# Moving the sample group's loads and all stores of results and gates from SyncE's queue to GpSimd's

## The chip, the cores and the metric

The kernel runs on one core of a Trainium2 chip. The metric is the device time of one execution in microseconds (us). The kernel before took 2027.31 us, the median of three runs (2026.1 to 2027.38 us).

The core's engines appear under the names of the profile: PE is TensorE (matmuls; PEld is its weight load), DVE is VectorE, ACT is ScalarE, POOL is GpSimd, and SP is SyncE, which computes nothing and here issues nearly all DMA transfers. "SPq" marks a transfer issued by SP. Each engine works through its own list of instructions in order.

## What is computed

One step of a one-layer hybrid decoder, for a prompt of 256 tokens and, with the same weights, 8 samples of one token each: 264 columns in all, with a model width of 2048.

```
h     = rmsnorm(x);  proj = h @ w_in          # three mixers and three merge gates
o_r   = RWKV-7 time mixing   (16 heads x 64)
o_m   = mLSTM matrix memory  (4 heads x 256)
o_g   = gated linear attention, GLA (4 heads, 128 x 256)
gates = sigmoid(proj_gate + gate_b)           # 3 x 2048 per token
x     = x + sum(gates * (o_r, o_m, o_g each @ w_branch)) @ w_out
x     = x + (silu(g) * u) @ ffn_w_down        # g, u = halves of rmsnorm(x) @ ffn_w_gu
y     = rmsnorm(x)
```

For the samples each mixer starts from a state in memory and gives back the state after one token: RWKV S (16 x 64 x 64 per sample), mLSTM C (4 x 256 x 256), GLA S (4 x 128 x 256). All is float32.

## The kernel before, in words

**Weights.** Every matrix is packed on the host into one stream `wst`, cut into units of mostly 4 x 128 rows by 256 columns (512 KB). `weights` loads a unit into `raw` (L331, SP), ScalarE rounds it into `wh` (L334), VectorE makes the remainder `wl = raw - wh` (L257, a helper that records every two-input operation of VectorE). `raw`, `wh` and `wl` have three buffers each. `unit` then issues 24 matmuls for a full unit (L266, also a helper): `wh` times the high part of the activations, `wh` times the low part, `wl` times the high part. These three steps of a weight unit are marked as of high priority.

**Order of the work.** The code is written for Tile, a framework that assigns semaphores and whose scheduler puts the instructions of each engine in order before the kernel runs, by priority (the order in the code, with the marked ones ahead) and by when it expects them to be ready. So an instruction can stand on its engine well before or after its place in the code. On the chip that order is fixed.

**Background work.** The mixers are written as generators. `unit` calls `fill` after each half of a unit; `fill` moves the prompt's mixers on by a step and, every second call (every fourth from the FFN on), one generator of `bg`, the sample group's work. In `fill` the kernel before also issues the stores that have been put on the list `stores` since the last call.

**The transfers that the change touches.**

- `load` (L369, SP): the samples' loads. In the sample stage: `Ss` from the RWKV states, `Ct` from the mLSTM states, `St` from the GLA states (all in six shared buffers, tag `ct`), and `qb` and `gqb`, rows of queries broadcast to all partitions. In the FFN part: `Cb` and `kb` (in new_C), `Sb` and `kgb` (in new_S), `Ss` (in new_W).
- `store`: puts a transfer on the list; `fill` issues it a step later (L379, SP). So go the gates (`g_d` from `sgate`, 24 times), the mixers' outputs (`o_d`), the prompt's new states and small results.
- Stores written out directly (SP): `o_cs`, `o_sh`, `o_cv`, and the samples' new states `o_sC` (L1471), `o_sg` (L1486), `o_swkv` (L1506).

Weight loads, the loads of `of`, `sgl` and `xr` for the merge, the blocks of the RWKV inverse (`nd`, `xd`) and the final `yT` stay on SP.

**Renewing the states.** `later` runs new_C 16 times (four heads, pairs of samples), new_S 16 times, new_W 8 times. A job of new_C: loads `Cb` (three buffers) and `kb` (two); four scaled copies into `kv` on ScalarE (L263; `kv` has two buffers); two fused multiply-adds on VectorE (L260); the store of `kv` to `o_sC`. A job of new_S: loads `Sb` (three buffers) and `kgb` (two); a product into `Sb` on POOL (L1480); four scaled copies into `kvg` on ScalarE; one addition on VectorE; the store to `o_sg`. A job of new_W loads `Ss`, works on it with POOL (L1500, `tms`) and VectorE, and stores it to `o_swkv`.

**Other POOL work.** In the sample stage POOL makes the products `tms` (L860) and, for the prompt's GLA heads, the differences `gd` (L1195), from which ScalarE and VectorE make the operands `gsc` of the score matmuls. In the projection part it copies small pieces, such as `bonS` (L642).

Of the kernel before, what the change touches and what calls it, by code (L numbers as in the profile page):

```python
# [247 lines left out]
def body(tc, a, stop=None):  # L248
    nc = tc.nc
# [3 lines left out]
    def sb(name, bufs=1, **kw):  # L253
        return tc.tile_pool(name=name, bufs=bufs, **kw)

    def tt(out, x, y, op):
        vec.tensor_tensor(out=out, in0=x, in1=y, op=op)  # L257
# [4 lines left out]
    def af(out, x, f, bias=0.0, scale=1.0):  # L262
        act.activation(out=out, in_=x, func=f, bias=bias, scale=scale)  # L263
# [6 lines left out]
    with ctx:  # L270
# [20 lines left out]
        cvT = const.tile([P, 16, 3, B], F32, name="cvT")  # L291
# [5 lines left out]
        sh_o = const.tile([P, 26, 9], F32, name="sh_o")  # L297
        cv_o = const.tile([P, 16, 11], F32, name="cv_o")

        def V(n, i=0, w=1):  # L300
            return vecs[:, VEC[n] + i:VEC[n] + i + w]

        def NVv(n, i=0, w=1):
            o = {"gb": 0, "w0": 48, "a0": 56, "ka": 64}[n] + i
            return nvec[:, o:o + w]
# [57 lines left out]
                unit(name, ps, k0, nk, hi, lo, kof)  # L363
            return ps

        mix, bg, tick, stores, every = {}, [], [0], [], [2]

        def load(out, in_):
            nc.sync.dma_start(out=out, in_=in_)  # L369

        def store(out, in_):

            stores.append((out, in_))

        def fill():

            now, stores[:] = stores[:], []
            for o, i in now:
                nc.sync.dma_start(out=o, in_=i)  # L379
            for lane in list(mix):  # L380
                while mix[lane] and next(mix[lane][0], 0) == 0:
                    mix[lane].pop(0)
                if not mix[lane]:
                    del mix[lane]
            tick[0] += 1
            if tick[0] % every[0] == 0:
                step(1)

        def step(n):
            while n and bg:  # L390
                g = bg.pop(0)
                if next(g, 0) is None:
                    bg.append(g)
                    n -= 1
# [91 lines left out]
        def setup():  # L486

            lw = ip.tile([P, BW], F32, tag="xs", name="lw", bufs=5)
            lgw = ip.tile([64, BW], F32, tag="xs", name="lgw", bufs=5)
            gf = ip.tile([P, len(LV), P], F32, tag="xs", name="gf", bufs=5)  # L490
            for t, n in ((lw, "lw"), (lgw, "lgw"), (cvT, "cvT"), (nT, "nT"), (mT, "mT"), (ga, "ga"), (gf, "gm")):
                nc.sync.dma_start(out=t, in_=a[n])
            for n, w in (("gb", 48), ("w0", 8), ("a0", 8), ("ka", 8)):
                vec.tensor_scalar(out=NVv(n, 0, w), in0=V(n, 0, w), scalar1=-1.0, scalar2=None, op0=MUL)

            for i, src, hh, hl in ((0, lw[H0], H0, H1), (1, lw[H1], H1, H0), (2, lgw, H0, H1)):
                act.copy(out=LW[i][hh], in_=src)
                tt(LW[i][hl], src, LW[i][hh].bitcast(F32), SUB)
            act.activation(out=identR, in_=ones[:, 0:4], func=AF.Copy, scale=0.0)
            for t, n in ((onesR, ones), (bonesR, bones), (cenR, cen), (identR[0:4], ident[0:4, 0:4]), (identR[32:36], ident[32:36, 32:36])):  # L500
                act.copy(out=t, in_=n)
            for j in range(3):
                w = V("cw", 16 * j, 16).unsqueeze(2).to_broadcast([P, 16, B])
                if j == 0:
                    tt(cvS, cvT[:, :, 0, :], w, MUL)
                else:
                    tmp = ip.tile([P, 16, B], F32, name="tmp")
                    tt(tmp, cvT[:, :, j, :], w, MUL)
                    tt(cvS, cvS, tmp, ADD)
            tt(cvS, cvS, V("cb", 0, 16).unsqueeze(2).to_broadcast([P, 16, B]), ADD)  # L510
            nc.sync.dma_start(out=a["o_cs"], in_=cvT[:, :, 1:3, :])
            pool.tensor_copy(out=gm, in_=gf)
            zero = ip.tile([P, 520], F32, name="zero")
            pool.memset(zero, 0.0)
            for q in range(4):
                for i in range(2):
                    nc.sync.dma_start(out=xd[q][i][0:66560].rearrange("(p f) -> p f", p=P), in_=zero)
            ictx.close()
# [535 lines left out]
        def row(t, o, ap):  # L1054

            return bass.AP(tensor=t.tensor, offset=t.offset + o, ap=[[0, P]] + ap)
# [302 lines left out]
        for name, _, _, _ in groups[1:]:  # L1359
            if name[0] == "r" and name[1] == 0:  # L1360
                r_group(name[2])
                if name[2] == 0:
                    mp = mctx.enter_context(sb("m", side="right"))
                    mix.setdefault("m", []).append(m_gates())
            elif name[0] == "m" and name[1] == 0:
                m_group(name[2])
            elif name[0] == "g":
                if gp is None:
                    nc.sync.dma_start(out=a["o_sh"], in_=sh_o)
                    nc.sync.dma_start(out=a["o_cv"], in_=cv_o)  # L1370
                    while mix or stores:
                        fill()
                    rctx.close()
                    mctx.close()
                    gp = gctx.enter_context(sb("g"))
                    sp = gctx.enter_context(sb("s"))
                    bg += [r_sample(), m_sample()]
                g_part(*name[1:])
            elif name[0] == "gate":
                if name in trail:  # L1380
                    break
                gate(*name[1:])
        while mix or bg or stores:
            fill()
        gctx.close()

# [69 lines left out]
        def new_C(h, b):  # L1456
            Cb = fp.tile([P, 2, 2, 256], F32, name="Cb", bufs=3)
            load(Cb, a["mC"][h, :, b:b + 2])
            kb = fp.tile([P, 2, 256], F32, name="kb", bufs=2)
            load(kb, row(rk_d, BW * b + 256 * h, [[BW, 2], [1, 256]]))  # L1460
            yield
            kv = fp.tile([P, 2, 2, 256], F32, name="kv", bufs=2)
            for i in range(2):
                for j in range(2):
                    af(kv[:, i, j, :], kb[:, i, :], AF.Identity, scale=vS[:, 0, 2 * h + j, b + i:b + i + 1])
            yield
            for i in range(2):
                if i:
                    yield
                stt(kv[:, i], Cb[:, i], scS[:, h, b + i:b + i + 1], kv[:, i], MUL, ADD)  # L1470
            nc.sync.dma_start(out=a["o_sC"][h, :, b:b + 2], in_=kv)  # L1471

        def new_S(h, b):
            Sb = fp.tile([P, 2, 2, P], F32, name="Sb", bufs=3)
            load(Sb, a["gS"][h, :, b:b + 2])
            kb = fp.tile([P, 2, 2, P], F32, tag="kb", name="kgb", bufs=2)
            load(kb, row(rg_d, 1536 * b + 384 * h + 128, [[1536, 2], [1, 256]]))
            yield
            kv = fp.tile([P, 2, 2, P], F32, tag="kv", name="kvg", bufs=2)
            pool.tensor_tensor(out=Sb, in0=Sb, in1=kb[:, :, 1:2, :].to_broadcast([P, 2, 2, P]), op=MUL)  # L1480
            for i in range(2):
                for j in range(2):
                    af(kv[:, i, j, :], kb[:, i, 0, :], AF.Identity, scale=vS[:, 1, 2 * h + j, b + i:b + i + 1])
            yield
            tt(kv, kv, Sb, ADD)
            nc.sync.dma_start(out=a["o_sg"][h, :, b:b + 2], in_=kv)  # L1486

        def new_W(v0):
            S = fp.tile([P, 8, 64], F32, tag="Sb", name="Ss", bufs=3)
            load(S, a["wkv"][:, v0:v0 + 8, :])  # L1490

            def along(j):
                return natR[:, j:j + 1, :].to_broadcast([P, 8, 64])

            def col(x):
                return x[:, v0:v0 + 8].unsqueeze(2).to_broadcast([P, 8, 64])

            yield
            tm = fp.tile([P, 8, 64], F32, tag="kb", name="tms", bufs=2)
            pool.tensor_tensor(out=tm, in0=along(5), in1=col(uR), op=MUL)  # L1500
            tt(S, S, along(1), MUL)
            yield
            tt(S, S, tm, SUB)
            tt(tm, along(2), col(natR[:, 3, :]), MUL)
            tt(S, S, tm, ADD)
            nc.sync.dma_start(out=a["o_swkv"][:, v0:v0 + 8, :], in_=S)  # L1506

        def later():
            yield from pipeline(new_C(h, b) for h in range(4) for b in range(0, B, 2))
# [63 lines left out]
```

## Time and profile before

| | us |
|---|---|
| median of three runs | 2027.31 |
| the profiled execution | 2026.99 |
| its span, first to last instruction | 2025.3 |
| PE busy | 1957.6 |
| DVE busy | 1336.6 |
| ACT busy | 1042.1 |
| POOL busy | 166.9 |

The span is what the trace's times count in. Matmuls are pipelined: one of 264 columns shows a duration of some 285 ns, but the next one starts before it ends, so a group's sum of durations says nothing, and the busy time of a stretch divided by its matmuls does. The parts of the kernel follow each other in the span about so: projections with the RWKV and mLSTM mixers of the prompt to 640 us; GLA of the prompt and all mixers of the samples to 950 us; the merge of the branches to 1130 us; the output projection to 1237 us; the FFN to the end. The granted TensorE clock over the whole run is 0.994 of full speed.

### The profile page before, as it was taken

How to read it: one execution, taken by the hardware profiler on the slowest of the kernel's cores; microseconds unless marked ns; L12 is line 12 of the kernel's file. 1: busy time of each engine (PE TensorE's matmuls, PEld its weight loads, DVE VectorE, ACT ScalarE, POOL GpSimd, SP SyncE). 2: the span in 40 equal slices, each digit the busy share in tenths (PEclk: the TensorE clock that was granted, in tenths of full speed). 3: DMA queues.
4: the chain of work that ended last, by engine and by line, in shares of the span. 5: the costliest groups of instructions: out<-in, count | busy, mean ns of one | idle time of the engine just before them, and what ended most of it. 6: DMA issues, size and time to landing. Idle time of an engine off the chain costs nothing.

```text
span 2025.3 us, 41016 instructions
## 1 busy us (share of the span) xinstructions
PE 1957.6 (97%) x16526; PEld 1913.3 (94%) x16526; DVE 1336.6 (66%) x2382; ACT 1042.1 (51%) x1700; POOL 166.9 (8%) x257
## 2 busy tenths in 40 slices
PE   7999999999999899999999999998999999999997
PEld 7899999999998889989999999988999999999997
DVE  7777776767766878776566666568654455555554
ACT  5755655755755355566444566554443344444443
POOL 5110100100100311110000000123000000000000
PEclk9999999999999999999999999999999999999999
DMA  7563554554454778558777898987655555555554
GB/s 256 180 184 128 172 174 142 166 171 151 163 171 145 242 279 275 176 175 271 224 227 221 281 309 303 300 299 260 202 179 177 183 187 180 184 178 185 174 182 137
DMA packets 173526, 414.89 MB, mean 205 GB/s; under 512 B 47512, under 2 KB 69432, under 8 KB 173336
## 3 DMA queue, kind: packets, MB, share of 16 engines
q1 hardware_dynamic: 172904, 411.53, 62.3%
q8 instruction: 129, 2.11, 0.4%
q10 hardware_dynamic: 432, 0.74, 0.1%
q14 instruction: 61, 0.50, 0.1%
HBM read 379.61 MB, written 32.61 MB: 204 GB/s over the span
## 4 chain that ended last, share of the span: by engine, by line
PE 67%; DMA 12%; DVE 9%; ACT 7%; issue 4%; SPq 1%; POOL 1%; DVEq 0%; ACTq 0%; POOLq 0%
PE ps L266 61%; PE mx L266 5%; DVE wl L257 4%; DMA o_sC<-kv 4%; ACT wh L334 3%; DMA kgb<-rg_d 2%; DVE dot L840 1%; DMA of<-o_d 1%; DMA Ss<-wkv 1%; ACT sg L263 1%; DMA raw<-wst 1%; ACT sgate L263 1%; DMA gqb<-rg_d 1%; DMA o_swkv<-Ss 1%; DMA St<-gS 0%
## 5 line engine op out<-in xcount | busy, mean ns | idle before, releaser
L257 DVE TENSOR_TENSOR wl<-raw,wh 128x1024 fp32r<-128x1024 f32 (+2 forms) x613 | 747.9, 1222 | 470.3 <-ACT wh L334 464.9
L334 ACT CAST wh<-raw 128x1024 fp32r<-128x1024 f32 (+2 forms) x613 | 631.9, 1033 | 605.6 <-PE ps L266 521.6
L266 PE MATMUL ps<-xh,wh 128*128 128x264 f32 x2080 | 608.9, 293 | 7.2 <-ACT wh L334 6.9
L266 PE MATMUL ps<-xh,wl 128*128 128x264 f32 x2080 | 596.8, 287 | 16.0 <-DVE wl L257 15.8
L266 PE MATMUL ps<-xl,wh 128*128 128x264 f32 x2080 | 593.9, 286 | 0.0
L266 PE MATMUL ps<-gh,wl 128*128 128x264 f32 x1408 | 401.7, 285 | 13.8 <-DVE wl L257 13.7
L266 PEld LDWEIGHTS ps<-xh,wl 128*128 128x128 f32 x2080 | 393.7, 189 | 21.5 <-DVE wl L257 19.9
L266 PEld LDWEIGHTS ps<-xh,wh 128*128 128x128 f32 x2080 | 395.2, 190 | 12.5 <-ACT wh L334 7.6
L266 PE MATMUL ps<-gh,wh 128*128 128x264 f32 x1408 | 400.7, 285 | 2.1 <-ACT wh L334 2.1
L266 PE MATMUL ps<-gl,wh 128*128 128x264 f32 x1408 | 399.3, 284 | 0.0
L266 PEld LDWEIGHTS ps<-xl,wh 128*128 128x128 f32 x2080 | 395.5, 190 | 0.9
L266 PEld LDWEIGHTS ps<-gh,wl 128*128 128x128 f32 x1408 | 264.3, 188 | 18.9 <-DVE wl L257 18.9
L266 PEld LDWEIGHTS ps<-gh,wh 128*128 128x128 f32 x1408 | 264.9, 188 | 3.3 <-ACT wh L334 3.3
L266 PEld LDWEIGHTS ps<-gl,wh 128*128 128x128 f32 x1408 | 265.1, 188 | 0.0
L266 PE MATMUL ps<-al,wh 128*128 128x264 f32 x704 | 200.3, 285 | 0.0
L266 PE MATMUL ps<-ah,wh 128*128 128x264 f32 x704 | 200.1, 284 | 0.0
L266 PE MATMUL ps<-ah,wl 128*128 128x264 f32 x704 | 199.7, 284 | 0.0
L266 PEld LDWEIGHTS ps<-ah,wl 128*128 128x128 f32 x704 | 133.0, 189 | 0.0
L266 PEld LDWEIGHTS ps<-al,wh 128*128 128x128 f32 x704 | 132.2, 188 | 0.0
L266 PEld LDWEIGHTS ps<-ah,wh 128*128 128x128 f32 x704 | 132.1, 188 | 0.0
L266 PE MATMUL ps<-oh,wh 128*128 128x264 f32 x384 | 109.0, 284 | 0.0
L266 PE MATMUL ps<-oh,wl 128*128 128x264 f32 x384 | 108.9, 284 | 0.0
(406 smaller groups left out, 2366.8 us busy)
## 6 DMA issues: line engine op xcount, KB each, us to landing
raw<-wst SPq DMA_DIRECT2D x579, 512.0 KB, 3.5
raw<-wst SPq DMA_DIRECT2D x32, 384.0 KB, 3.1
Ct<-mC SPq DMA_DIRECT2D x16, 512.0 KB, 5.1
Cb<-mC SPq DMA_DIRECT2D x16, 512.0 KB, 6.7
o_sC<-kv SPq DMA_DIRECT2D x16, 512.0 KB, 6.3
g_d<-sgate SPq DMA_DIRECT2D x24, 264.0 KB, 4.4
sgl<-g_d SPq DMA_DIRECT2D x24, 264.0 KB, 3.6
qb<-rq_d SPq DMA_DIRECT2D x4, 1024.0 KB
```

The source lines that it names most:

```text
L257: vec.tensor_tensor(out=out, in0=x, in1=y, op=op)
L263: act.activation(out=out, in_=x, func=f, bias=bias, scale=scale)
L266: pe.matmul(out, lhsT=lhsT, rhs=rhs, start=start, stop=stop)
L334: act.copy(out=wh[:, 0:nk, :], in_=raw[:, 0:nk, :])
L840: vec.tensor_tensor_reduce(out=tm[:, 0:x.shape[1]], in0=x, in1=y, scale=1.0, scalar=0.0, op0=MUL, op1=ADD, accum_out=out)
```

## The change

`load` issues on GpSimd's queue. `store` is the same function: it issues at once, on GpSimd's queue, and no list is kept. The stores that were written out on SP call `store`.

```
-        mix, bg, tick, stores, every = {}, [], [0], [], [2]
+        mix, bg, tick, every = {}, [], [0], [2]
 
         def load(out, in_):
-            nc.sync.dma_start(out=out, in_=in_)
-
-        def store(out, in_):
-
-            stores.append((out, in_))
+
+            nc.gpsimd.dma_start(out=out, in_=in_)
+
+        store = load
 
         def fill():
 
-            now, stores[:] = stores[:], []
-            for o, i in now:
-                nc.sync.dma_start(out=o, in_=i)
             for lane in list(mix):
...
-            nc.sync.dma_start(out=a["o_cs"], in_=cvT[:, :, 1:3, :])
+            store(a["o_cs"], cvT[:, :, 1:3, :])
...
-                    nc.sync.dma_start(out=a["o_sh"], in_=sh_o)
-                    nc.sync.dma_start(out=a["o_cv"], in_=cv_o)
-                    while mix or stores:
+                    store(a["o_sh"], sh_o)
+                    store(a["o_cv"], cv_o)
+                    while mix:
                         fill()
...
-        while mix or bg or stores:
+        while mix or bg:
             fill()
...
-            nc.sync.dma_start(out=a["o_sC"][h, :, b:b + 2], in_=kv)
+            store(a["o_sC"][h, :, b:b + 2], kv)
...
-            nc.sync.dma_start(out=a["o_sg"][h, :, b:b + 2], in_=kv)
+            store(a["o_sg"][h, :, b:b + 2], kv)
...
-            nc.sync.dma_start(out=a["o_swkv"][:, v0:v0 + 8, :], in_=S)
+            store(a["o_swkv"][:, v0:v0 + 8, :], S)
```

## Rows read from the trace of the kernel before

**Rows 1.** The page's first part: the span, and each engine's busy time.

```profile
span 2025.3 us, 41016 instructions
...
PE 1957.6 (97%) x16526; PEld 1913.3 (94%) x16526; DVE 1336.6 (66%) x2382; ACT 1042.1 (51%) x1700; POOL 166.9 (8%) x257
```

**Rows 2.** Busy us by stretch: length, PE, PEld, DVE, ACT, POOL, clock, DMA, GB/s.

```profile
1500.00:2000.00 500.00, 500.00 (x4119) 500.00 (x4119) 261.24 (x312) 209.33 (x253) 0.00 (x0) 1.00 0.55 181
100.00:640.00 540.00, 538.69 (x5084) 514.86 (x5083) 392.48 (x849) 321.66 (x585) 41.83 (x130) 1.00 0.50 159
640.00:950.00 310.00, 289.63 (x2303) 282.82 (x2303) 234.45 (x602) 159.96 (x303) 51.88 (x52) 0.98 0.71 234
1130.00:1290.00 160.00, 153.75 (x1228) 150.01 (x1227) 106.27 (x150) 98.70 (x176) 0.00 (x0) 1.00 0.91 307
1290.00:1420.00 130.00, 118.43 (x936) 114.43 (x934) 91.85 (x119) 64.82 (x121) 37.80 (x24) 1.00 0.85 281
```

**Rows 3.** Waits, 640 to 950 us: who for whom, us, times, longest.

```profile
PE ps L266 <- DVE wl L257: 9.7, 8, 3.0
PE mx L266 <- DVE gsc L257: 6.1, 5, 3.3
...
ACT wh L334 <- DMA raw<-wst: 29.5, 13, 8.1
```

**Rows 4.** An issue of SP, a piece of the chain, the page's weight loads.

```profile
663.50 0.38 SPq L369 DMA_DIRECT2D qb<-rq_d  x1
...
667.58 7.66 DMA raw<-wst
...
raw<-wst SPq DMA_DIRECT2D x579, 512.0 KB, 3.5
```

**Rows 5.** new_C: a wait, one late store in four timeline rows, the page's median.

```profile
ACT kv L263 <- DMA o_sC<-kv: 39.2, 13, 4.6
...
1200.62 0.74 DVE L260 SCALAR_TENSOR_TENSOR kv<-Cb,scS,kv 128x512 f32<-128x512 f32 x1
...
1209.39 0.33 SPq L331 DMA_DIRECT2D raw<-wst  x1
1209.77 0.42 SPq L1471 DMA_DIRECT2D o_sC<-kv  x1
...
1215.48 0.91 ACT L263 ACTIVATE kv<-kb,vS 128x256 f32<-128x256 f32 x2 [1.67 <-DMA o_sC<-kv]
...
o_sC<-kv SPq DMA_DIRECT2D x16, 512.0 KB, 6.3
```

**Rows 6.** 1290 to 1420 us: a wait of ACT, one of SP, the chain.

```profile
ACT kvg L263 <- DMA kgb<-rg_d: 26.1, 12, 3.5
...
SPq L369 <- DMA o_swkv<-Ss: 12.3, 5, 3.6
...
1318.20 1.24 DVE wl L257
...
1320.36 5.44 DMA kgb<-rg_d
```

**Rows 7.** Cb's issues (ns min/median/max, first and last start), and ACT's first `rs` of the FFN.

```profile
L369 SPq DMA_DIRECT2D Cb<-mC x16: 423/466/857, 1126.5 to 1268.4; - x16
...
1237.17 0.47 ACT L263 ACTIVATE rs<-mx,vecs 128x264 f32<-128x264 f32 x1
```

**Rows 8.** POOL: a small copy (busy us, mean ns), and new_S's products by stretch.

```profile
L642 POOL COPY bonS<-bon 128x8 f32<-128x8 f32 x8 | 7.4, 920 | 2.9 <-DMA raw<-wst 1.6 <-DVE bon L257 0.9
...
1290.00:1380.00 90.00, 22.88 (x16) 1.00 0.88 288
```

**Rows 9.** The dots on DVE (ns min/median/max), and one beside POOL's work.

```profile
L840 DVE CUSTOM_DVE_ANT_0 dot<-Ct,qb x64: 402/414/2616, 679.4 to 810.0; 128x256 f32<-128x256 f32 x64
...
697.65 2.62 DVE L840 CUSTOM_DVE_ANT_0 dot<-Ct,qb 128x256 f32<-128x256 f32 x1
...
696.67 5.84 POOL L860 TENSOR_TENSOR tms<-Ss,natR 128x1024 f32<-128x1024 f32 x2 [6.18 <-DMA Ss<-wkv]
```

## The prediction

> **What bounds the kernel now.** I read the page's first part, then the busy time by stretch, then the waits of the stretches that have idle time, and last SP's issues beside the chain of waits. TensorE is busy for 1957.6 us of a span of 2025.3 us [rows 1]; what can be won is its idle time, and the stretches say where that lies [rows 2]. From 1500 to 2000 us there is none: 4119 matmuls at 500/4119 = 0.121 us. From 100 to 640 us there are 540 - 538.69 = 1.3 us. Three stretches hold the rest that the change can touch, and in all three the moved transfers run beside the weights: the sample stage, 640 to 950 us, idles 310 - 289.63 = 20.4 us; the stretch in which the mLSTM states are renewed (new_C, 1130 to 1290 us) 160 - 153.75 = 6.25 us; that of new_S and new_W (1290 to 1420 us) 130 - 118.43 = 11.6 us. Together 38 us, 1.9% of the time. The remaining 28 us or so stand at the start and the end, where almost nothing is moved.
>
> In the sample stage TensorE waits 9.7 us for `wl` and 6.1 us for the gate scores of GLA; ScalarE waits 29.5 us for raw weights [rows 3]. The longest such wait can be followed [rows 4]: SP issues the 1 MB broadcast `qb` at 663.50; the weight load issued at 667.58 takes 7.66 us on the chain, where the median weight load lands in 3.5 us. It queued behind `qb` on the same queue.
>
> In the new_C stretch ScalarE waits 39.2 us, 13 times, for the store `o_sC` to give back a `kv` buffer [rows 5]. The rows show why the store is late. The second product of a job starts at 1200.62 and is done at 1201.36; its store is issued at 1209.77. In between SP, which works in order, stands at a weight load that it can issue only at 1209.39, when `wl` of an earlier unit has been made. At 1215.48 the store has landed (6.3 us is the median), and ScalarE starts the job that has waited 1.67 us for that buffer. So there is a ring: store lands, `kv` on ScalarE, `wh` behind it, `wl`, the weight load's issue on SP, the next store behind that. One turn takes about 9.5 us and TensorE falls short a little on each.
>
> The third stretch has the same ring with `kgb` in the store's place: ScalarE waits 26.1 us for it, and on the chain a `wl` of 1.24 us stands ahead of a `kgb` load of 5.44 us. In addition SP itself stands 12.3 us at L369, for stores of `o_swkv` to land, with weight loads queued behind [rows 6].
>
> **The change part by part.** *What moves.* By the loops: 108 loads (16 each of Ct, Cb, kb, Sb, kgb, 12 Ss, 8 St, 4 qb, 4 gqb), 77 issues of `store` at L379 (24 of gates among them) and 43 direct stores (16 o_sC, 16 o_sg, 8 o_swkv, o_cs, o_sh, o_cv), 228 in all. An issue holds SP for 0.42 us [rows 5], at the median of Cb 0.466 us [rows 7]; with 0.43 us, 98 us come off SP. I cost that at nothing by itself: SP's time is mostly waiting, and from 1500 to 2000 us, where nothing is moved, it feeds TensorE without a gap.
>
> *What POOL pays.* Before, POOL issues no DMA, so the price of one is bounded: below by SP's 0.43 us, above by 1.43 us, a whole product Sb (22.88/16). I take 0.92 us, a copy of eight elements a partition [rows 8], the nearest POOL instruction whose time is hardly data. That adds 228 x 0.92 = 210 us to POOL's 167 us: 19% of the span in place of 8%. Tightest is new_S, 16 jobs in 90 us [rows 8], 5.6 us each: 1.43 + 3 x 0.92 = 4.2 us, and 5.7 us at the upper price, when POOL is just full.
>
> *New_C.* The store goes out when the product is done: 1201.36 + 0.92, and with 6.3 us to land the buffer is free by 1208.6; ScalarE asks for it at 1213.8 (1215.48 less its wait of 1.67). Slack 5 us even if landing stays as it is; at POOL's upper price 4.7 us. The ring opens. Next late is the `kb` and `Cb` pair, two and three jobs ahead, which SP's weight loads no longer hold. I take 6 of the 6.25 us.
>
> *New_S and new_W.* Opening the ring takes SP's turn (a `wl` and a weight load's issue, 1.24 + 0.33 us) out of a `kgb` turn, and the waits for `o_swkv` leave SP. But `kgb` has two buffers and must still land, and now POOL's own product Sb, which waits for `kgb`, stands ahead of the loads and stores queued behind it. I take 7 of 11.6 us.
>
> *Sample stage.* Weight loads no longer follow 1 MB and 512 KB loads on one queue. Bounds for such a load: 3.5 us, the median, to 7.66 us as now. I take 7 of the 9.7 us. The 6.1 us for GLA's scores stay: they begin on POOL, at `gd`, and some 60 of the moved transfers stand on that queue. Where a store now waits on POOL for ScalarE or VectorE to finish (stores are no longer put off a step), what is queued behind it is `gd` and `tms`, and behind these `gsc` on VectorE and the scores on TensorE. I charge 3 us (bounds 0 to 10: 60 x 0.92 = 55 us of POOL, shared out over 310 us of which POOL works 52), and 2 us for the hand-over to the `of` loads, which need the last stores landed.
>
> *First 640 us and the end.* POOL's small copies and memsets wait behind stores there; the mixers run many steps behind the projections and the idle time is 1.3 us. Without that slack each store would cost its 0.92 us. Nothing moved stands near the end. I take 0, bounds 0 and +5 us.
>
> **Sum**: -6 - 7 - 7 + 3 + 2 = -15 us. The profiled execution took 2026.99 us, 1.7 us beyond its span and 0.3 us under the median of the runs. 2027.31 - 15 gives 2012 us.
>
> What SP does to the store at 1209.77 is 8.4 us of standing in line and 0.42 us of issue [rows 5]; the sum above rests on the first. A rule speaks against a gain: the Trainium skill, "DMA: Bandwidth & Descriptors", section Issuing engines are not separate DMA queues, says that the DMAs of all engines end on the same 16 DMA engines, and that issuing from several saves only issue time. By that rule the sum would be 0, the first rival below.
>
> **The rivals.** *No change.* The landings carry the stalls: in new_C the DMA engines are 91% busy, in new_S and new_W 85% [rows 2]. Half a microsecond more per issue on the rings of 32 new_C and new_S jobs is up to 16 us, which eats the gain. Against it: 8.4 us of the new_C ring are SP's, not the landing's. 2024 to 2031 us, chance 0.15.
>
> *POOL's issuing holds VectorE: slower.* The trace shows that the two hold each other: a `dot`, 414 ns at the median, takes 2.62 us at 697.65 while POOL works on `tms` from 696.67 [rows 9]. If writing a transfer's descriptors does the same for 0.92 us, the 112 moved transfers of 1130 to 1420 us take 103 us of VectorE. It is busy 106.27 + 91.85 = 198 us there [rows 2], so 301 us are wanted in 290: VectorE becomes the bound, 11 us over, and with some 60 transfers in the sample stage (234 + 55 of 310 us) another 5 or so. It decides from (290 - 198)/112 = 0.82 us a transfer. About 2043 us, chance 0.14. Against it: `tms` reads two whole tiles, a DMA issue reads none.
>
> The Trainium skill, "SBUF — State Buffer", section SBUF: two separate sides, lets a VectorE operation with two SBUF inputs exclude only a GpSimd operation that reads SBUF, and warns that VectorE in a two-port mode locks GpSimd out of writing descriptors. By that rule `wl` would not be held; nothing in the trace before tests it.
>
> *A denser order: slower.* The engines' orders come from the framework's scheduler: the first Cb load is issued at 1126.5 us, though the code puts it inside the gate-and-up loop, whose first `rs` runs at 1237.17 [rows 7]. With SP free it may pack one new_C job onto two weight units (2 x 24 x 0.121 = 5.8 us) instead of about three. That is 1.31 MB moved (512, 256 and 512 KB) plus 1.05 MB of weights, 407 GB/s, where 307 GB/s are 91% of the engines: full, 337. So 7.0 us a job, 1.2 us of idle time x 16 = 19 us against 6.25 now, and later landings in new_S. About 2035 us, chance 0.10. Against it: two `kv` buffers and the stores' landing limit the scheduler as well.
>
> **How the numbers follow.** A measurement of this kernel tells about 0.2%, 4 us, from no change. My forecast, 1998 to 2023 us, has 0.61; its lower end is all of 9.7 + 6.25 + 11.6 us won at no cost, 1999.8, and a little of GLA's waits. The range goes on to 2043 us, the second rival's price; what is left out is worse than that, or better than 1998 us. Faster 0.61, within 0.2% 0.15, slower 0.14 + 0.10 = 0.24.
>
> **What would show it.** Right: ScalarE's wait for `o_sC` in new_C falls from 39 us to a few; SP's issues are weight loads and little else; ScalarE's longest wait for raw weights is under 5 us; TensorE idles under 1 us in new_C. Wrong: VectorE's `wl` longer than the 1.24 us of [rows 6] wherever POOL issues; POOL issues of over 1.4 us with `Sb` late; DMA shares above 0.95 with TensorE idle in new_C; or the same wait of ScalarE on a store that was issued in time.

## The result, and the profile after

The changed kernel takes 2087.49 us (median of four runs, 2084.4 to 2093.77) where the kernel before takes 2026.7 us beside it: a ratio of 1.0301, 95% interval 1.0283 to 1.032. It is slower by 61 us; 15 us of gain had been forecast. The profiled execution took 2093.77 us, the slowest of the four.

The page's first part and some of its DMA issues (KB each, median us to landing):

```profile
span 2091.7 us, 41167 instructions
...
PE 1989.6 (95%) x16526; PEld 1944.6 (93%) x16526; DVE 1349.6 (65%) x2382; ACT 1043.6 (50%) x1700; POOL 298.9 (14%) x485
...
raw<-wst SPq DMA_DIRECT2D x579, 512.0 KB, 3.4
...
Ct<-mC POOLq DMA_DIRECT2D x16, 512.0 KB, 10.4
Cb<-mC POOLq DMA_DIRECT2D x16, 512.0 KB, 9.6
o_sC<-kv POOLq DMA_DIRECT2D x16, 512.0 KB, 7.9
```

The span is 66.4 us longer than in [rows 1]. TensorE is busy for 32.0 us more with the same 16526 matmuls, so they ran more slowly, and it idles 102.1 us in place of 67.7. The busy time by stretch, as in [rows 2], says where:

```profile
640.00:950.00 310.00, 282.24 (x2187) 275.12 (x2186) 229.14 (x590) 150.29 (x290) 93.03 (x120) 0.96 0.68 220
...
1130.00:1290.00 160.00, 133.12 (x939) 126.93 (x937) 94.09 (x131) 90.65 (x183) 55.32 (x82) 0.91 0.91 312
1290.00:1420.00 130.00, 109.58 (x794) 106.96 (x795) 88.76 (x112) 53.05 (x89) 42.19 (x54) 0.90 0.68 215
...
1420.00:1700.00 280.00, 280.00 (x2308) 280.00 (x2307) 143.92 (x168) 111.28 (x127) 0.00 (x0) 1.00 0.56 181
```

Count matmuls, which weigh idle time and slow clock alike. The sample stage does 116 fewer than in [rows 2]; new_C, new_S and new_W do 1228 + 936 - 939 - 794 = 431 fewer. At 0.121 us that is 14 and 52 us: the whole 66 us by which the span grew.

**What became of new_C and new_S.** The next view is the busy time of ScalarE's weight casts alone (x counts them), then clock, DMA share and GB/s. First the kernel before, while its stores `o_sC` and then `o_sg` go out:

```profile
1135.00:1285.00 150.00, 48.44 (x47) 1.00 0.90 307
1292.00:1380.00 88.00, 27.51 (x27) 1.00 0.88 290
```

The same two stages in the changed kernel:

```profile
1148.00:1244.00 96.00, 23.81 (x23) 0.89 0.98 359
1244.00:1342.00 98.00, 20.93 (x21) 0.86 0.76 234
```

The work on the samples' states has been packed among fewer weight units, in new_C among half as many. (The stretches take in a cast or two more at their edges than the counts that follow.) In ScalarE's order, which is fixed before the kernel runs, 46 weight casts stand between the first and the last scaled copy into `kv`, and 26 for `kvg`; in the changed kernel 23 and 19. So 16 jobs of new_C pass in 96 us instead of 150, with the DMA engines 98% busy; but the 23 weight units of that time are 23 x 24 x 0.121 = 67 us of TensorE's work, and 29 us are lost there against a TensorE at full speed; in the kernel before 47 such units left 13.5 us of 150. In the 98 us of the second row it is 21 x 24 x 0.121 = 61 us of work, and 37 us are lost.

Three rows of the changed kernel's timeline show that the store is no longer late:

```profile
1159.30 1.41 DVE L260 SCALAR_TENSOR_TENSOR kv<-Cb,scS,kv 128x512 f32<-128x512 f32 x2
...
1161.70 0.56 POOL L370 DMA_DIRECT2D o_sC<-kv  x1
...
1164.70 0.51 ACT L263 ACTIVATE kv<-kb,vS 128x256 f32<-128x256 f32 x1 [5.37 <-DMA o_sC<-kv]
```

The products end at 1160.71, and the store goes out 0.99 us later, where SP had taken 8.4 us [rows 5]. ScalarE waits for an earlier `o_sC` all the same, 5.37 us: the landing has become the wait. The waits from 1140 to 1400 us:

```profile
POOL kb L370 <- ACT kv L263: 51.5, 13, 8.2
...
ACT kvg L263 <- DMA o_sg<-kvg: 40.6, 10, 7.6
...
PE ps L266 <- ACT wh L334: 28.0, 14, 7.4
ACT kv L263 <- DMA o_sC<-kv: 25.5, 8, 5.9
...
PE ps L266 <- DVE wl L257: 19.2, 23, 2.1
```

ScalarE's order has `kv` and `kvg` ahead of the weight casts; it stands at them, and TensorE waits for `wh` behind. In new_S the two `kvg` buffers are given back by `o_sg`, for which before nobody waited.

**The clock.** Busy time by 3 us of the changed kernel; the first x counts matmuls, the clock is third from the right:

```profile
1182.00:1185.00 3.00, 2.76 (x23) 2.55 (x22) 0.00 (x0) 0.08 (x1) 0.00 (x0) 1.00 1.03 421
1185.00:1188.00 3.00, 0.53 (x2) 0.30 (x2) 1.96 (x3) 2.57 (x5) 0.14 (x1) 0.86 1.02 410
1188.00:1191.00 3.00, 2.93 (x13) 2.93 (x14) 2.48 (x5) 2.61 (x6) 1.65 (x3) 0.50 0.88 303
1191.00:1194.00 3.00, 3.00 (x16) 3.00 (x15) 3.00 (x7) 3.00 (x7) 0.00 (x0) 0.50 0.85 200
1194.00:1197.00 3.00, 3.00 (x26) 3.00 (x26) 1.03 (x2) 0.06 (x1) 1.80 (x3) 1.00 1.01 396
```

TensorE did two matmuls in 1185 to 1188 us. Then it was granted 0.50, the lower level of 1.2 GHz, for 6 us, and did 13 and 16 matmuls where 26 fit. So a long stall costs twice. The clock accounts for TensorE's 32 us of extra busy time: it was 0.91 and 0.90 from 1130 to 1420 us, where it had been 1.00, and 0.96 in place of 0.98 in the sample stage, by an estimate 0.09 x 160 + 0.10 x 130 + 0.02 x 310 = 34 us.

**Sample stage.** GpSimd's timeline from 662 us:

```profile
662.51 0.56 POOL L370 DMA_DIRECT2D rk_d<-vr  x1
663.06 0.56 POOL L370 DMA_DIRECT2D Ss<-wkv  x1
663.62 0.50 POOL L370 DMA_DIRECT2D rk_d<-vr  x1
664.11 0.92 POOL L370 DMA_DIRECT2D qb<-rq_d  x1
665.02 0.55 POOL L370 DMA_DIRECT2D Ct<-mC  x1
```

And two pieces of the chain of waits (start, us):

```profile
665.02 13.98 DMA Ct<-mC
699.88 9.24 DMA raw<-wst
```

Loads leave in a bunch as soon as buffers and queue allow. The `Ct` of 665.02 takes 13.98 us to land, and a weight load on its own queue still takes 9.24 us, beside `Ct` and `qb` loads issued in the same microseconds. The waits of the stage, 640 to 950 us:

```profile
PE ps L266 <- DVE wl L257: 13.0, 8, 4.2
PE mx L266 <- DVE gsc L257: 10.3, 5, 3.0
...
ACT wh L334 <- DMA raw<-wst: 46.7, 12, 11.7
```

All three have grown [rows 3]: 9.7 to 13.0, 6.1 to 10.3 and 29.5 to 46.7 us.

### The profile page after: what moved, and what is told of

It reads as the page before. It is cut to its first block, busy times and chain, and to the rows that moved or that the text cites. A ratio compares the mean times of both kernels' runs of the same rounds, so it can differ in the third digit from the quotient of the medians.

```text
span 2091.7 us, 41167 instructions
## 1 busy us (share of the span) xinstructions
PE 1989.6 (95%) x16526; PEld 1944.6 (93%) x16526; DVE 1349.6 (65%) x2382; ACT 1043.6 (50%) x1700; POOL 298.9 (14%) x485
## 4 chain that ended last, share of the span: by engine, by line
PE 71%; DMA 11%; DVE 6%; ACT 5%; issue 5%; POOL 1%; DVEq 0%; SPq 0%; POOLq 0%; ACTq 0%
PE ps L266 65%; PE mx L266 5%; DMA o_sC<-kv 2%; DVE wl L257 2%; ACT wh L334 2%; DMA kgb<-rg_d 2%; DMA raw<-wst 2%; DMA gqb<-rg_d 1%; DVE dot L836 1%; DMA o_sg<-kvg 1%; DMA Ss<-wkv 1%; ACT sg L263 1%; DMA Ct<-mC 1%; DMA kb<-rk_d 1%; POOL Sb L1476 0%
## 5 line engine op out<-in xcount | busy, mean ns | idle before, releaser
L257 DVE TENSOR_TENSOR wl<-raw,wh 128x1024 fp32r<-128x1024 f32 (+2 forms) x613 | 756.3, 1235 | 532.5 <-ACT wh L334 527.8
L266 PE MATMUL ps<-gh,wh 128*128 128x264 f32 x1408 | 406.7, 289 | 18.7 <-ACT wh L334 18.7
L266 PEld LDWEIGHTS ps<-xh,wl 128*128 128x128 f32 x2080 | 398.7, 192 | 23.0 <-DVE wl L257 21.4
L266 PE MATMUL ps<-gh,wl 128*128 128x264 f32 x1408 | 406.7, 289 | 10.5 <-DVE wl L257 10.5
L266 PEld LDWEIGHTS ps<-xh,wh 128*128 128x128 f32 x2080 | 400.0, 192 | 11.7 <-ACT wh L334 7.1
L266 PE MATMUL ps<-gl,wh 128*128 128x264 f32 x1408 | 405.0, 288 | 0.0
L266 PEld LDWEIGHTS ps<-gh,wh 128*128 128x128 f32 x1408 | 271.2, 193 | 20.2 <-ACT wh L334 20.2
L266 PEld LDWEIGHTS ps<-gh,wl 128*128 128x128 f32 x1408 | 270.4, 192 | 13.1 <-DVE wl L257 13.0
L266 PEld LDWEIGHTS ps<-gl,wh 128*128 128x128 f32 x1408 | 271.3, 193 | 0.0
## 6 DMA issues: line engine op xcount, KB each, us to landing
Ct<-mC POOLq DMA_DIRECT2D x16, 512.0 KB, 10.4
```

What stands on the lines that cost most here:

```text
L266: pe.matmul(out, lhsT=lhsT, rhs=rhs, start=start, stop=stop)
```

## The experiments

The theory: **order**. GpSimd's queue opens the ring as predicted, but the framework's scheduler, seeing another queue, packs the samples' transfers more densely, and that loses more than the ring gave. The rivals: **GpSimd's queue itself** is the cost (its issuing, its slower landings, what waits behind a waiting transfer), at any order; or the loss lies in the **sample stage**. Every kernel is compared with the kernel before, run beside it.

| kernel | us | ratio (95%) | casts at `kv` / `kvg` |
|---|---|---|---|
| e1 FFN part on SP | 2037.08 | 1.0058 (1.0038 to 1.0079) | 46 / 26 |
| e2 only the FFN part on GpSimd | 2072.93 | 1.0248 (1.0228 to 1.0267) | 23 / 19 |
| e3 change, FFN part tied, every 6 | 2009.95 | 0.9933 (0.9916 to 0.9951) | 48 / 45 |
| e4 the same, every 4 | 2051.69 | 1.0138 (1.0112 to 1.0163) | 32 / 30 |
| e6 the same, every 3 | 2071.82 | 1.0251 (1.0218 to 1.0284) | 24 / 23 |
| e5 before, loads tied, every 6, SP | 2040.71 | 1.0081 (1.0066 to 1.0096) | 45 / 45 |
| e7 e3, tied from the sample stage | 2024.44 | 0.9996 (0.9979 to 1.0012) | 48 / 45 |
| e8 sample loads on SP, stores untied | 2071.68 | 1.0237 (1.0202 to 1.0273) | 45 / 45 |
| e11 e3, FFN stores untied | 2080.57 | 1.027 (1.0238 to 1.0301) | 45 / 45 |
| e9 before, FFN part on GpSimd, tied, every 6 | 2013.9 | 0.9945 (0.9927 to 0.9962) | 48 / 45 |
| e12 the same, every 8 | 2027.76 | 1.0011 (0.9994 to 1.0028) | 64 / 61 |
| e10 e3, sample loads on SP | 2011.25 | 0.9925 (0.99 to 0.9951) | 48 / 45 |
| e13 e3, sample stores on SP, later | 2025.23 | 0.9986 (0.9971 to 1.0001) | 48 / 45 |
| e14 e3, sample stores on GpSimd, later | 2020.66 | 0.9961 (0.9946 to 0.9976) | 48 / 45 |

### Which part loses: e1 and e2

e1 is the changed kernel with `later`'s transfers back on SP, at once; e2 is the kernel before with only `later`'s transfers on GpSimd.

```
+        eng = [nc.gpsimd]                    # e2: [nc.sync]
         def load(out, in_):
-            nc.gpsimd.dma_start(out=out, in_=in_)
+            eng[0].dma_start(out=out, in_=in_)
...
         bg.append(later())
+        eng[0] = nc.sync                     # e2: nc.gpsimd
```

In e2 the three stores of `later` call `load` as well.

> The changed kernel, but with the loads and stores of new_C, new_S and new_W on SP again; only what lies ahead of the FFN is on GpSimd. ScalarE's order is that of before there (46 weight casts between the first and the last kv of new_C, 23 in the changed kernel). Density theory (the scheduler packs the background work onto half as many weight units once SP is free, and the DMA engines and the landings can't follow): the loss of the FFN part goes, some 17 us of the sample stage stay, about 2044 us. POOL-path theory (transfers issued by GpSimd land later and hold whoever waits for them): much the same here, 2040 to 2050 us; this run only splits the loss between the stages.

> The kernel before, with the loads and stores of new_C, new_S and new_W alone on GpSimd. The order there is the changed kernel's (23 casts in new_C, 19 in new_S). If the two parts of the loss add up, about 2027 + 45 = 2072 us, by both theories; under 2040 us would say that the loss comes from the stages ahead of it.

e1 took 2037.08 us, 11.7 over the kernel before beside it (2025.34); e2 2072.93, 47.6 over. Together 59 us, near the change's 61: two losses that add up. The stretches 640 to 950 and 1130 to 1420 us of e1:

```profile
640.00:950.00 310.00, 282.52 (x2240) 276.59 (x2239) 234.29 (x596) 156.02 (x296) 93.33 (x121) 0.97 0.68 228
1130.00:1420.00 290.00, 275.82 (x2190) 269.21 (x2189) 198.15 (x268) 164.74 (x298) 35.68 (x24) 0.99 0.89 300
```

And of e2:

```profile
640.00:950.00 310.00, 289.21 (x2308) 282.70 (x2308) 235.19 (x602) 160.76 (x303) 50.73 (x52) 0.98 0.71 235
1130.00:1420.00 290.00, 246.92 (x1802) 236.91 (x1801) 185.47 (x247) 149.15 (x277) 95.94 (x131) 0.93 0.79 272
```

Each has at least the matmuls of the kernel before where its transfers are on SP (2303, and 1228 + 936 = 2164 [rows 2]) and fewer where they are on GpSimd. The orders follow the queue too: 46 and 26 casts in e1, 23 and 19 in e2. "At once" on SP does not pack them; the queue's choice does.

### Queue or order: e3, e5, e4, e6

A transfer of the FFN part is tied to the latest weight cast in the code: it may not stand before it in the order, and no time is added on the chip. `fill` moves the samples' work on every sixth call. So GpSimd's queue stays, and the dense packing goes.

```
+                cast[0] = act.copy(out=wh[:, 0:nk, :], in_=raw[:, 0:nk, :])
...
-            nc.gpsimd.dma_start(out=out, in_=in_)
+            d = nc.gpsimd.dma_start(out=out, in_=in_)
+            if pin[0]:
+                tc.add_manual_dep(d.ins, cast[0].ins.name, mybir.DependencyInfo(
+                    mybir.DependencyClass.NoSync, mybir.DependencyReason.DATA), reason="pace")
...
-        every[0] = 4
+        every[0] = 6
+        pin[0] = True
```

e5 does the same to the kernel before: its `load` ties the loads, on SP, and the stores stay as they were. e4 and e6 are e3 with `every[0]` 4 and 3.

> The changed kernel, all on GpSimd, but each load of new_C, new_S and new_W may be placed by the scheduler only behind the weight cast that stands ahead of it in the code, and a step is made every six half units in place of four: 48 casts in new_C and 45 in new_S. No wait on the chip is added. Density theory: the FFN part costs nothing any more, TensorE idles under 8 us from the first kv on, 2035 to 2046 us. POOL-path theory: the landings are as late as in the changed kernel and hold ScalarE at every step, above 2065 us.

> The kernel before, all on SP, with the same pacing (45 casts in new_C, 45 in new_S). It is the counterpart of the run before it: same pace, other queue. Density theory: as before or a little faster, 2012 to 2028 us, since new_S is spread out as well; its difference to the paced GpSimd kernel is then the sample stage's 17 us and nothing from the FFN part. POOL-path theory: the difference is 40 us or more, most of it in the FFN part.

> As the paced GpSimd kernel (2010 us), but a step every four half units: 32 casts in new_C and 30 in new_S, two weight units a job in place of three. Density theory: new_C wants 2.36 MB in 5.8 us, 407 GB/s where 337 to 365 GB/s have been seen, so some 10 to 19 us of idle time come back, and a lower clock after it: 2020 to 2040 us. If something else in the pacing than the density made the gain (the place of the jobs behind the gate-and-up loop's start, the tie itself), it stays at 2008 to 2014 us.

> The same, with a step every three half units: 24 casts in new_C and 23 in new_S, almost the changed kernel's 23 and 19, at a place of the program that the tie still fixes. Density theory: most of the FFN part's loss is back, 2050 to 2075 us. If the tie or the place made the gain: 2008 to 2020 us.

e3 took 2009.95 us: 15.4 us faster than the kernel before and 77 us faster than the change, with all 228 transfers still on GpSimd's queue. Its stretches:

```profile
640.00:950.00 310.00, 284.86 (x2251) 277.87 (x2250) 234.02 (x598) 156.89 (x298) 93.41 (x121) 0.97 0.69 228
...
1130.00:1420.00 290.00, 289.16 (x2381) 288.68 (x2380) 186.39 (x247) 162.98 (x262) 43.42 (x67) 1.00 0.80 272
```

From 1130 to 1420 us TensorE idles 0.8 us and does 2381 matmuls; the DMA share is 0.80, and `o_sC` lands in 6.1 us, as before the change. In no row of ScalarE's waits does `o_sC` stand any more. What still waits is GpSimd, where nobody minds:

```profile
POOL kb L372 <- ACT kv L263: 182.5, 14, 93.2
```

e5, with nearly the same casts but on SP, took 2040.71 us, 31 us more than e3. Loads are late in it (waits of ScalarE and of SP from 950 us on):

```profile
ACT kvg L263 <- DMA kgb<-rg_d: 70.1, 16, 7.2
...
ACT kv L263 <- DMA kb<-rk_d: 40.8, 14, 5.3
...
SPq L1491 <- DVE kvg L257: 58.8, 13, 6.8
```

But the queue is not all that differs: e3's stores are tied, e5's are not. The last row is a store, `o_sg`, that stands on SP until its product is made, with weight loads and the next `kgb` load behind it. From 1380 to 1560 us, where it stands, e5 does 1294 matmuls and e3 1484, which is 23 us. In new_C, 1210 to 1380 us, where SP stands for `o_sC` only 4.8 us, they do 1309 and 1399: 11 us. (In the sample stage, still on SP, e5 is 9 us ahead; behind 1560 us it loses about as much.) So the rows put about 11 us down to weight loads on the same queue, the prediction's reason for a gain; the rest goes with the untied store, and no run with the FFN part on SP has its stores tied.

The dose settles the order's part on GpSimd's queue: 48 casts at `kv` give 2010 us, 32 give 2052, 24 give 2072, all tied, with new_C starting at the same place (1223 to 1230 us). e6 has as few casts as the change in new_C and as large a loss as e2, though some 9 us of it are the sample stage's (2229 matmuls). What binds is not the same in all of them, though. In e4's new_S it is a ring on GpSimd itself:

```profile
1391.25 0.71 POOL L372 DMA_DIRECT2D kgb<-rg_d  x1
1397.05 1.29 POOL L1481 TENSOR_TENSOR Sb<-Sb,kgb 128x512 f32<-128x512 f32 x1 [5.09 <-DMA kgb<-rg_d]
...
1399.39 0.71 POOL L372 DMA_DIRECT2D kgb<-rg_d  x1
```

The product `Sb` waits on GpSimd for its `kgb` to land, and the next loads stand behind it. A turn takes 8 us, where 30 casts for 16 jobs are 5.4 us of matmuls. At e3's 45 casts, 8.2 us a job, GpSimd waits in the same way, but TensorE is busy for all 180 us from 1380 to 1560 us. So the cost at a dense order is partly what stands in GpSimd's queue, and the two theories meet there. A dense order on SP's queue was not run.

### The sample stage: e7 to e10, e13, e14

e7 sets `pin[0]` when the samples' generators start, so that their loads and stores are tied too. e8 and e10 put the loads up to the FFN on SP again; in e8 `store` lost its tie thereby, in e10 it keeps it. e9 is the kernel before up to the FFN, stores a step later on SP, and e3 behind it; e12 is e9 with `every[0] = 8`. e13 and e14 are e3 with the old list for the stores up to the FFN, issued in `fill` on SP and on GpSimd.

```
                     bg += [r_sample(), m_sample()]
+                    pin[0] = True                                                # e7
...
-            d = nc.gpsimd.dma_start(out=out, in_=in_)
+            d = (nc.gpsimd if pin[0] else nc.sync).dma_start(out=out, in_=in_)   # loads: e8, e9, e10, e12
...
+            (load if pin[0] else lambda o, i: stores.append((o, i)))(out, in_)   # store: e13, e14
...
+            now, stores[:] = stores[:], []
+            for o, i in now:
+                nc.sync.dma_start(out=o, in_=i)                                  # e14: nc.gpsimd
```

> The paced GpSimd kernel, with the tie from the sample stage on. The order of the sample stage was not denser in the changed kernel (33 remainders wl over the 64 dots on Ct, 32 before; 37 here), so density is not the cause there. If the sample stage's loss is GpSimd's issuing as soon as a buffer is free, a few loads at once, this changes little: 2003 to 2012 us. If it is the scheduler's order there too: 1998 to 2004 us.

> The paced GpSimd kernel, with the sample stage's loads (Ss, Ct, qb, gqb, St) back on SP; all stores, and the loads of the FFN part, stay on GpSimd. If the loads make the sample stage's loss (they collide with the weights when they are issued as soon as a buffer is free): 2000 to 2005 us, and ScalarE's longest wait for raw weights in the stage falls from about 11 us to about 8. If the stores make it (GpSimd stands at a store while gd and tms wait behind it): 2008 to 2013 us.

> Sample stage and all stores up to the FFN as before (SyncE, a step later); only the transfers of new_C, new_S and new_W on GpSimd, tied to every sixth fill. If the change's loss has two separate parts, the scheduler's denser order in the FFN part and 6 to 14 us of GpSimd's transfers in the sample stage, this keeps the gain of the first (2010 us in the tied run) and loses the second: 1998 to 2006 us, with about 2310 matmuls in 640 to 950 us. If the sample stage costs nothing by its queue, 2010 us again.

> The tied kernel with the samples' loads of the sample stage back on SyncE; its stores and gates stay on GpSimd at once, and all FFN transfers stay tied. If the loads in bursts are what costs in the sample stage: 1998 to 2006 us. If it is the gates and stores on GpSimd's queue: 2010 us, with 2240 to 2260 matmuls in 640 to 950 us as before.

> As the first kernel of this job, at eight fills a step instead of six: 64 and 61 casts a stage in place of 48 and 45. If the DMA share is what is left to win at six, the rest of the idle time in the FFN part goes: up to 5 us faster than the first kernel. If six is already enough, the same within 4 us.

> The tied kernel (2010 us), but up to the FFN the gates and other stores go a step later on SyncE, as before; the sample stage's loads stay on GpSimd. If the stores in GpSimd's queue, with gd and tms behind them, are the sample stage's cost: 2300 to 2320 matmuls in 640 to 950 us, and 2003 to 2006 us. If it is the loads in bursts, or the FFN's own order decides the rest: 2240 to 2260 matmuls and 2008 to 2014 us.

> The tied kernel, but up to the FFN the gates and other stores go a step later, on GpSimd. It undoes 'at once' alone. If waiting stores at the head of GpSimd's queue cost: matmuls in 640 to 950 us rise from 2251 to about 2300 and GpSimd's 171 us of waits for the gates fall to under 60. If not: 2240 to 2260 matmuls, and 2008 to 2014 us.

Matmuls in 640 to 950 us tell the stage's cost apart from what follows. With the whole stage on SP: 2303 (before), 2308 (e2), 2310 (e9), 2323 (e12), 2325 (e5). With any of it on GpSimd: 2187 (the change), 2199 (e4), 2229 (e6), 2231 (e11), 2240 (e1), 2251 (e3). Loads alone back on SP: 2251 (e8), 2263 (e10). Stores alone back: 2226 (e13). "At once" undone: 2249 (e14). Tying the stage's loads and stores: 2157 (e7, which at 2024.44 us has lost all of e3's gain). No kernel of the one kind reaches the other, so against the kernel before the stage costs 40 to 146 matmuls, 5 to 18 us; but no single part gives it back, and which wait carries it **stays open**. Late weight loads are not all of it: in e10 ScalarE's waits for them fall to 15.9 us, the longest to 5.0, and the stage has 12 matmuls more than e3's.

e9 has the sample stage back in full, and yet its 2013.9 us are not under e3's. It gains 7 us there and loses 10 us from 1420 to 1700 us, with 2207 matmuls against e3's 2292. VectorE's wait from 1500 to 1640 us, in e9:

```profile
DVE Ss L257 <- DMA Ss<-wkv: 21.3, 4, 7.2
```

In e3 that is 6.5 us. e13 and e14 show the same as e9 (2210 and 2207 matmuls). An edit upstream can thus give another result downstream, and such differences are not small: e12, with 64 casts, is 14 us slower than e9, although the DMA share from 1130 to 1420 us is only 0.71; why was not found. So differences of 10 to 15 us between two of these kernels don't by themselves show what an edit is worth.

### A store at the head of the queue: e11

e8's FFN part had lost 60 us with 45 casts a stage, which the order's density can't explain. e11 is e3 with only the stores untied.

```
-        store = load
+        def store(out, in_):
+
+            nc.gpsimd.dma_start(out=out, in_=in_)
```

> The tied kernel with only the stores of new_C, new_S and new_W free to stand where the scheduler likes. If an early store at the head of GpSimd's in-order queue holds the loads behind it: 2060 to 2075 us at an unchanged 45 casts a stage, with ScalarE waiting some 70 us each for kb and kgb loads. If it was the sample stage's loads on SyncE that cost in the earlier mixed run: 2010 us.

It took 2080.57 us, 71 more than e3. Waits from 950 us on:

```profile
POOL o_sC L379 <- DVE kv L260: 237.6, 16, 95.1
...
ACT kvg L263 <- DMA kgb<-rg_d: 75.4, 15, 9.7
ACT kv L263 <- DMA kb<-rk_d: 74.3, 13, 7.6
```

Free of the tie, a store stands on GpSimd ahead of loads whose buffers are free, waits there for its product, and the loads behind it are late. So in-order standing costs on GpSimd just as on SP; a queue helps only by what does not stand in it. This could be a rival for the change itself, whose stores are not tied either. Its trace speaks against it: from 1140 to 1400 us GpSimd waits 7.3 us at `o_sC` and 2.2 us at `o_sg`, and e6, with every store tied, loses as e2 does.

## Why the prediction was wrong

- **What bounds the kernel, and the ring: right as a reading of the kernel before.** The late store was SP's doing: 8.4 us of standing in line became 0.99. SP issues weight loads and little else. ScalarE's wait for `o_sC`, which was to fall from 39.2 us to a few, fell only to 25.5. That e3 comes within half a microsecond of the forecast (-15.4 us for -15) is luck: it also spreads new_S and ties the stores, so its FFN part gains 25 us by the matmuls where 13 were forecast, and its sample stage loses 6 where a gain of 2 was forecast.
- **POOL's price: a little high.** 0.92 us was taken. GpSimd's rows (busy us, mean ns; then the idle time before) give 0.56 us for most, and the 1 MB broadcast at the price taken:

```profile
L370 POOL DMA_DIRECT2D g_d<-sgate x24 | 13.4, 560 | 171.0 <-ACT sgate L263 171.0
...
L370 POOL DMA_DIRECT2D o_sC<-kv x16 | 8.9, 557 | 7.4 <-DVE kv L260 7.3
...
L370 POOL DMA_DIRECT2D qb<-rq_d x4 | 3.6, 910 | 6.1 <-DVE num L836 3.1 <-DVE gnum L836 3.0
```

- **New_C, -6 us, and new_S, -7 us: the step that failed.** The sum moved the transfers and kept the engines' orders: "The ring opens", with "landing stays as it is". In place of that the order was packed from 46 and 26 casts to 23 and 19, `o_sC` landed in 7.9 us instead of 6.3, and the 13 us of gain became 52 us of loss.
- **The rival "A denser order"** named the mechanism and the place, and two of the signs of being wrong that came fit it (a DMA share above 0.95 with TensorE idle; the same wait on a store issued in time). It had a chance of 0.10. Its price of 19 us was too low for three reasons. It took two weight units a job; there were 23 for 16 jobs, 1.4. With 1.4 its own sum gives 31 us, by an estimate (2.06 MB at 337 GB/s are 6.1 us a job, less 4.2 us of matmuls, 16 times), and new_C lost 29. It priced new_C alone; new_S was packed too, and there two `kvg` buffers and the landing of `o_sg` bound it, at a DMA share of 0.76. And it left out the clock, through which the same matmuls kept TensorE busy for 32 us more over the whole run. What spoke against it, that two `kv` buffers and the landing limit the scheduler as well, did not hold. The order is known before any run; one should have weighed that a move to another queue is a new schedule.
- **Sample stage, -7 + 3 us: wrong sign.** 14 us of loss. The term that failed is the -7: TensorE's wait for `wl` was to fall from 9.7 us and rose to 13.0, and ScalarE's longest wait for raw weights was to fall under 5 us and was 11.7. That a weight load of 7.66 us "queued behind `qb` on the same queue" was read into the rows: off that queue one still took 9.24 us. The 3 us charged for GLA's scores were about right, 10.3 for 6.1 us. What carries the stage's loss stays open, as said above.
- **"No change": the rule behind it is half right.** By the Trainium skill, "DMA: Bandwidth & Descriptors", section Issuing engines are not separate DMA queues, a second issuing engine saves issue time only. Once packed, new_C hits the shared limit the rule speaks of: 359 GB/s at a share of 0.98. But issue time is not all that a queue is about: a store held back 8.4 us behind a weight load made ScalarE wait in the kernel before, stores standing in GpSimd's queue cost e11 71 us, and an issue takes longer on GpSimd than on SP (0.557 against 0.426 us for `o_sC`).
- **"POOL's issuing holds VectorE": fell.** `wl` took 1235 ns at the mean, 1222 before, and VectorE was busy 13 us more over the whole run, where the rival wanted 103 us in two stages alone.

## What to carry to other kernels

Where a scheduler orders the engines, moving transfers to another queue is two changes: the queue and the order. Count, in the fixed order, how many units of the main work stand beside the side work before and after; if the count falls, work out the DMA rate that it asks for and what the main engine does meanwhile. To keep the order spread, tie the side transfers to the main work at a pace that the DMA engines have room for (found by trial here: 48 casts were better than 32 and than 64), and tie the stores with the loads, since on an in-order queue a store that waits for its product holds the loads behind it.

## What was not expected of the hardware

- The lower clock followed a stall of TensorE of about 3 us and lasted 6 us (1188 to 1194 us), in which some 23 matmuls were lost, as many as in the stall. A shorter one was followed by it too: from 1150 to 1153 us TensorE was busy for 1.41 us, and from 1153 to 1156 us it was granted 0.50 to 0.52.
- The 16 DMA engines moved 359 GB/s at a share of 0.98 with loads and stores on two queues; a weight load then took 7.9 us to land (median, 1150 to 1200 us), against 6.2 in the same 50 us of the kernel before and 3.5 over the whole run.
- Two 512 KB loads from GpSimd's queue, `Ct` and `Cb`, took 10.4 and 9.6 us to land at the median, where on SP, by the page of the kernel before, they took 5.1 and 6.7 us. In e3, at a DMA share of 0.80, `Cb` still took 7.8 us; it cost nothing there, since the buffers were loaded well ahead.
